# Holding the sum-free gate and up products behind the last out-projection matmul, loading their fourth operand earlier, and evacuating token tiles in one VectorE operation

## The chip, the core and the metric

The program runs on one core of one Trainium2 chip, once per launch. Its five engines work side by side, each through a queue of its own: TensorE (PE, matmuls, with its weight loads shown as PEld), VectorE (DVE), ScalarE (ACT), GpSimd (POOL) and SyncE (SP), which here only issues DMAs. ACT and POOL issue DMAs too, from the queue that also holds their arithmetic. The metric is the device time of one execution in microseconds (us), and lower is better. The kernel before took 1679.59 us, the median of three runs (1676.99 to 1682.70).

## The reference

One encoder layer over 1280 tokens (256 of a prompt, 1024 of a sample) with 1024 features. Only the second half of the layer is touched by the change:

```python
    mix = jnp.concatenate([rmsnorm(a, mla_out_g), rmsnorm(b, na_out_g)], axis=-1)
    x = x + mix @ w_o
    h2 = rmsnorm(x, ffn_norm_g)
    x = x + (jax.nn.silu(h2 @ w_gate) * (h2 @ w_up)) @ w_down
```

Everything is fp32. `a` and `b` are the outputs of the two groups of attention heads, `w_o` is 1024 x 1024, and `w_gate` and `w_up` are 1024 x 2816.

## The kernel before, in words

The tokens lie in ten tiles of 128. Each fp32 operand of a matmul is split into a high and a low part, and one product is three matmuls (high by high, high by low, low by high: lines 110 to 112, `mm3`). The high part is a ScalarE cast, the low part a subtraction on VectorE (activations) or GpSimd (weights).

**Out-projection, tile by tile** (the loop at L879). For tile t, `mix_in(t + 1)` loads the attention outputs of the next tile, scales them (rstd and scaling on GpSimd), transposes them on TensorE into the bank `trm` and splits them into `mT`. `out_proj(t)` makes 48 matmuls into `po` (two halves of 512 columns, eight contraction chunks, three matmuls each) and adds them to the residual `x` on VectorE. `ffn_in(t)` squares `x` (ScalarE, L793), takes the rstd (GpSimd), scales (VectorE, L796), transposes eight 128 x 128 blocks into `trh` or `trm` (L805) and evacuates them with the gain `gf` into the four quarters `R["11"]`, `R["12"]`, `R["21"]`, `R["22"]`. The second digit of a quarter says whether the token tile is in the first five or the last five, the first digit which half of the features it holds.

**Gate and up products.** They are made by a Strassen-Winograd scheme with seven products per pair of weight blocks in the order `SEQ = (1, 2, 6, 7, 4, 5, 3)`. Product m takes a sum of activation quarters, `S[m]`, and a sum of weight blocks. Products 1 and 2 take no sum at all: `S[1]` and `S[2]` are quarters of tiles 0 to 4, and their weights are the blocks "11" and "12" as loaded. Product 6 takes `S[6]`, which is built from the sums `T2` of tiles 5 to 9 (`build_S(6)`, five cuts of 128 tokens), and the weight sum s2 = "21" + "22" - "11" (`operand`, L858). A product is twice twelve matmuls of 320 columns (`product`, two token halves s), for the gate (i = 0) and the up projection (i = 1). `finish` applies Silu to the gate, multiplies it by up and stores finished quarters to DRAM (`act_d`, from ScalarE's queue).

In the first pass (fp = 0, L963 to L983) three of the four sum-free weights are loaded and split in the loop over token tiles, at t == 6. The fourth (block "12" of up) and the blocks for the sums go into memory that the out-projection's pools have given back, so those six loads are issued when its last matmuls are done.

**What sets the order.** The program is traced in the order of the code, and a scheduler then orders each engine's instructions by its own simulation of when operands will be there. Every engine but SP is so ordered; SP keeps the order of the code. `tc.issue_after(ins)` adds the rule that what is traced under it stands behind `ins` on the engine of `ins`. Each engine then works strictly through its own list. In the list of before, 48 of the 96 matmuls of the sum-free products stand between out-projection matmuls and 48 behind the last one.

## Time and profile before

| | before |
|---|---|
| median of three runs | 1679.59 us |
| profiled execution, its own time | 1682.38 us |
| its span in the trace | 1680.6 us |
| PE busy in the span | 1612.6 us (96%) |
| DVE, ACT, POOL busy | 888.3, 724.6, 645.3 us |
| mean granted TensorE clock | 0.985 of full speed |

The profiled execution's own time is 1.8 us above its span, and 2.8 us above the median. In the trace, times are counted from the start of the span. A view of windows gives the busy time of each engine in a stretch with the number of its instructions, the granted clock of TensorE (1.00 is 2.4 GHz) and the mean busy share of the DMA engines. A timeline row gives start, duration, engine, line and the tiles written and read; a bracket at its end is the idle time of that engine just before it and what released it. A matmul's row lasts until its result has left the array, so the spacing of starts, not the duration, is what one costs in a dense run. The busy share says where an engine works but not whether it waits for anything at the end.

### The profile page before, as it was taken

The page shows a single profiled execution, that of the slowest core. Times are in us where ns is not written, and L with a number is a line of the kernel's source. Part 1 is how long each engine was busy: PE and PEld are TensorE (multiplying, and loading weights), DVE is VectorE, ACT ScalarE, POOL GpSimd, SP SyncE. Part 2 cuts the span into 40 slices and gives each one's busy share as a digit, 9 for nine tenths or more (in the row PEclk, how much of TensorE's full clock was granted, in tenths as well). Part 3 has the DMA queues.
Part 4 walks back from the last instruction along what each step waited for, and adds up shares of the span by engine and source line. Part 5 has one row for each costly group of instructions (what it writes and reads, how often), then busy time and mean ns, then how long its engine had stood idle before and what let it go on. Part 6 is the DMA issues. An engine that isn't in the chain of part 4 may idle for free.

```text
span 1680.6 us, 25657 instructions
## 1 busy us (share of the span) xinstructions
PE 1612.6 (96%) x9601; PEld 1455.7 (87%) x9601; DVE 888.3 (53%) x1521; ACT 724.6 (43%) x1500; POOL 645.3 (38%) x795
## 2 busy tenths in 40 slices
PE   7999999999899999999969999999999999999998
PEld 6987899987688888788869999999999997788886
DVE  4654045454677777443355443344444337865776
ACT  5433144454577777544443222332222233433434
POOL 3451435353011119223367565656656650000102
PEclk9999999999999999999979999999999999999999
DMA  6635302125001003233212321322332228733434
GB/s 223 199 101 144 75 21 60 36 96 163 20 19 34 20 29 98 76 125 136 85 45 91 106 81 62 102 86 93 106 101 72 71 79 329 269 94 94 142 107 149
DMA packets 123068, 169.78 MB, mean 101 GB/s; under 512 B 35328, under 2 KB 66944, under 8 KB 122944
## 3 DMA queue, kind: packets, MB, share of 16 engines
q1 hardware_dynamic: 78704, 118.99, 23.0%
q10 hardware_dynamic: 43680, 46.87, 8.1%
q0 software_dynamic: 560, 2.29, 0.4%
q8 instruction: 75, 1.23, 0.3%
q14 instruction: 49, 0.40, 0.1%
HBM read 117.65 MB, written 50.46 MB: 100 GB/s over the span
## 4 chain that ended last, share of the span: by engine, by line
PE 83%; issue 4%; DMA 3%; POOL 3%; DVE 3%; ACT 2%; SPq 0%; ACTq 0%; POOLq 0%; DVEq 0%
PE M L112 10%; PE M L110 10%; PE M L111 10%; PE d L111 5%; PE d L110 5%; PE d L112 5%; PE o L686 3%; PE tp L679 3%; PE po L110 2%; PE pj L110 2%; PE po L112 2%; PE po L111 2%; PE pj L111 2%; PE pj L112 2%; PE na_o L462 2%
## 5 line engine op out<-in xcount | busy, mean ns | idle before, releaser
L110 PE MATMUL M<-S,wc 128*128 128x320 f32 x1056 | 324.7, 312 | 9.6 <-ACT wc L845 9.5
L111 PE MATMUL M<-S,wc 128*128 128x320 f32 x1056 | 326.7, 311 | 0.0
L112 PE MATMUL M<-S,wc 128*128 128x320 f32 x1056 | 314.0, 311 | 0.7 <-POOL wc L846 0.7
L110 PEld LDWEIGHTS M<-S,wc 128*128 128x128 f32 x1056 | 199.8, 190 | 11.4 <-ACT wc L845 11.2
L111 PEld LDWEIGHTS M<-S,wc 128*128 128x128 f32 x1056 | 200.3, 190 | 0.3
L112 PEld LDWEIGHTS M<-S,wc 128*128 128x128 f32 x1056 | 196.5, 189 | 1.6 <-POOL wc L846 1.5
L846 POOL TENSOR_TENSOR wc<-A,wc 128x512 fp32r<-128x512 f32 x85 | 119.0, 1402 | 85.6 <-ACT wc L845 84.0
L111 PE MATMUL d<-w,ah 128*128 128x512 f32 x385 | 145.8, 397 | 2.5 <-DVE w L1016 2.5
L110 PE MATMUL d<-w,ah 128*128 128x512 f32 x385 | 143.4, 397 | 3.7 <-ACT ah L1015 3.7
L112 PE MATMUL d<-w,ah 128*128 128x512 f32 x385 | 143.7, 396 | 0.0
L916 DVE TENSOR_TENSOR z<-M,z 128x320 f32<-128x320 f32 x120 | 57.0, 488 | 141.7 <-PE M L112 131.3
L845 ACT CAST wc<-A 128x512 fp32r<-128x512 f32 x85 | 52.8, 622 | 167.2 <-PE M L111 145.9
L846 POOL TENSOR_TENSOR wc<-sum,wc 128x512 fp32r<-128x512 f32 x62 | 87.8, 1415 | 86.4 <-ACT wc L845 86.4
L916 DVE TENSOR_TENSOR zB<-M,zB 128x320 f32<-128x320 f32 x100 | 47.6, 488 | 133.3 <-PE M L112 126.7
L100 DVE TENSOR_TENSOR PT<-tp,PT 128x512 fp32r<-128x512 f32 (+1 forms) x144 | 93.0, 658 | 40.8 <-ACT PT L99 39.4
L1015 ACT CAST ah<-as 128x640 fp32r<-128x640 f32 x77 | 56.0, 727 | 120.7 <-issue 65.6
L845 ACT CAST wc<-sum 128x512 fp32r<-128x512 f32 x62 | 38.4, 619 | 149.8 <-PE M L111 104.1
L99 ACT CAST PT<-tp 128x512 fp32r<-128x512 f32 (+1 forms) x144 | 79.2, 565 | 42.3 <-PE tp L679 39.4
L110 PEld LDWEIGHTS d<-w,ah 128*128 128x128 f32 x385 | 72.4, 188 | 22.2 <-ACT ah L1015 4.8
L671 DVE TENSOR_REDUCE mm<-S 128x1 f32<-128x1024 f32 (+1 forms) x80 | 84.8, 1061 | 12.8 <-PE S L112 11.2
L1016 DVE TENSOR_TENSOR ah<-as,ah 128x640 fp32r<-128x640 f32 x77 | 64.1, 835 | 51.8 <-ACT ah L1015 51.8
L111 PEld LDWEIGHTS d<-w,ah 128*128 128x128 f32 x385 | 72.5, 188 | 20.5 <-DVE w L1016 2.9
(397 smaller groups left out, 3994.0 us busy)
## 6 DMA issues: line engine op xcount, KB each, us to landing
as<-act_d SPq DMA_DIRECT2D x77, 320.0 KB
act_d<-z ACTq DMA_DIRECT2D x35, 320.0 KB
act_d<-zB ACTq DMA_DIRECT2D x35, 320.0 KB
A<-in_w_gate_dram SPq DMA_DIRECT2D x42, 256.0 KB
A<-in_w_up_dram SPq DMA_DIRECT2D x41, 256.0 KB
x<-in_x_tm_dram SPq DMA_DIRECT2D x20, 512.0 KB
cT_d<-stg ACTq DMA_DIRECT2D x20, 320.0 KB
w<-in_w_down_dram SPq DMA_DIRECT2D x11, 512.0 KB
```

The lines of the kernel that those rows point to most:

```text
L99: i = nc.scalar.copy(out=hi, in_=ps)
L100: nc.vector.tensor_sub(out=lo, in0=ps, in1=hi)
L110: nc.tensor.matmul(out, lhsT=sh, rhs=mh, start=first, stop=False, **kw)
L111: nc.tensor.matmul(out, lhsT=sh, rhs=ml, start=False, stop=False, **kw)
L112: nc.tensor.matmul(out, lhsT=sl, rhs=mh, start=False, stop=last, **kw)
L671: nc.vector.reduce_max(out=nm[:, u:u + 1], in_=S, axis=AX.X, negate=True)
L679: nc.tensor.transpose(tp[:, j], ex[:, kt * P:(kt + 1) * P], ident)
L845: i0 = nc.scalar.copy(out=hi, in_=raw)
L846: i1 = nc.gpsimd.tensor_tensor(out=lo, in0=raw, in1=hi, op=ALU.subtract)
L916: nc.vector.tensor_add(out=o, in0=ps, in1=a)
L1015: nc.scalar.copy(out=o[:, 0], in_=raw)
L1016: nc.vector.tensor_sub(out=o[:, 1], in0=raw, in1=o[:, 0])
```

## The change

- `mm3` returns its last instruction, and `out_proj` returns the last matmul of the tile. The eight sum-free products of the first pass are traced under `tc.issue_after(last_mm)`, so none of them can stand between out-projection matmuls any more. All eight come first, and the `finish` of product 2 moves to the place behind product 6.
- The block "12" of up is loaded at t == 7, into the buffer that the gate's block "12" had. Of the six late loads the blocks "21" and "22" now come first and the two blocks "12" last (the second is loaded once more for its later sum).
- `ffn_in` writes the first feature half of a tile with one VectorE multiplication (128 x 4 x 128, the gain broadcast along the tokens) and the second half with four ScalarE activations, for all ten tiles. Before, tiles 0 to 4 used four ScalarE activations for the first half and four VectorE ones for the second, and tiles 5 to 9 used eight ScalarE activations, and eight VectorE operations that subtracted into the quarters "11" and "12" on the way.
- Those subtractions are now whole-tile operations on SBUF: `difference` makes "11" and T2, `differences` makes "12" and "21". For tiles 5 to 8 these are four GpSimd operations where two stood. For tile 9 they are on VectorE, and the last two are put behind `build_S(6)`.
- `build_S(6)` no longer waits for the last difference of tile 9, so its first four cuts can be split earlier.

```diff
--- before.py
+++ after.py
@@ -109,7 +109,7 @@
         kw = {"skip_group_check": True} if onto else {}
         nc.tensor.matmul(out, lhsT=sh, rhs=mh, start=first, stop=False, **kw)
         nc.tensor.matmul(out, lhsT=sh, rhs=ml, start=False, stop=False, **kw)
-        nc.tensor.matmul(out, lhsT=sl, rhs=mh, start=False, stop=last, **kw)
+        return nc.tensor.matmul(out, lhsT=sl, rhs=mh, start=False, stop=last, **kw).ins
 
 
     p1 = pool("p1")
@@ -782,9 +782,10 @@
             hs = slice(hf * 512, (hf + 1) * 512)
             ps = po.tile([P, 512], F32, name="po", bufs=2)
             for kc in range(KC):
-                mm3(ps, mT[:, 0, kc], mT[:, 1, kc], wo[kc][:, 0, hs], wo[kc][:, 1, hs],
-                    kc == 0, kc == KC - 1)
+                last = mm3(ps, mT[:, 0, kc], mT[:, 1, kc], wo[kc][:, 0, hs], wo[kc][:, 1, hs],
+                           kc == 0, kc == KC - 1)
             nc.vector.tensor_add(out=x[:, hs], in0=ps, in1=x[:, hs])
+        return last
 
     def ffn_in(t, x):
         h2 = rm.tile([P, D], F32, name="m", bufs=3)
@@ -803,30 +804,33 @@
             for i in range(4):
                 kc = 4 * q + i
                 nc.tensor.transpose(tr[q][:, i], h2[:, kc * P:(kc + 1) * P], ident)
-            for i in range(4):
-                s = gf[:, 4 * q + i:4 * q + i + 1]
-                o = R[f"{q + 1}{t // 5 + 1}"][:, i, cs]
-                if t < 5 and q:
-                    nc.vector.tensor_scalar(out=o, in0=tr[q][:, i], scalar1=s, scalar2=1.0,
-                                            op0=ALU.mult, op1=ALU.mult)
-                else:
-                    nc.scalar.activation(o, tr[q][:, i], AF.Copy, scale=s)
-                if t >= 5:
-
-                    d = R["12" if q else "11"][:, i, cs]
-                    nc.vector.scalar_tensor_tensor(out=d, in0=tr[q][:, i], scalar=s, in1=d,
-                                                   op0=ALU.mult, op1=ALU.subtract)
+            o = R[f"{q + 1}{t // 5 + 1}"]
+            if q == 0:
+                nc.vector.tensor_mul(out=o[:, :, cs], in0=tr[q],
+                                     in1=gf[:, 0:4].unsqueeze(2).to_broadcast([P, 4, P]))
+            else:
+                for i in range(4):
+                    nc.scalar.activation(o[:, i, cs], tr[q][:, i], AF.Copy,
+                                         scale=gf[:, 4 + i:5 + i])
         if t < 5:
             split_S(1, cs)
             split_S(2, cs)
             return
-        eng = nc.vector if t == NT - 1 else nc.gpsimd
         nm = ("A21", "A22", "sum", "sum", "A12")[t - 5]
         T2[t - 5] = rY.tile([P, 4, P], F32, name=nm, bufs=2 if nm == "sum" else 1)
-        eng.tensor_tensor(out=T2[t - 5], in0=R["22"][:, :, cs], in1=R["11"][:, :, cs],
-                          op=ALU.subtract)
-        return eng.tensor_tensor(out=R["21"][:, :, cs], in0=R["21"][:, :, cs], in1=T2[t - 5],
-                                 op=ALU.subtract).ins
+        eng = nc.vector if t == NT - 1 else nc.gpsimd
+        difference(eng, R["11"][:, :, cs], R["12"][:, :, cs], R["11"][:, :, cs])
+        difference(eng, T2[t - 5], R["22"][:, :, cs], R["11"][:, :, cs])
+        if t < NT - 1:
+            differences(eng, t)
+
+    def difference(eng, out, a, b):
+        eng.tensor_tensor(out=out, in0=a, in1=b, op=ALU.subtract)
+
+    def differences(eng, t):
+        cs = slice((t % 5) * P, (t % 5 + 1) * P)
+        difference(eng, R["12"][:, :, cs], R["22"][:, :, cs], R["12"][:, :, cs])
+        difference(eng, R["21"][:, :, cs], R["21"][:, :, cs], T2[t - 5])
 
 
 
@@ -883,8 +887,10 @@
             for m, i, b in ((1, 0, "11"), (2, 0, "12"), (1, 1, "11")):
                 A0[i][b] = load_A(i, 0, b)
                 w0[m, i] = operand(A0[i], m)
-        out_proj(t, *cur)
-        last = ffn_in(t, cur[1])
+        if t == 7:
+            A0[1]["12"] = load_A(1, 0, "12")
+        last_mm = out_proj(t, *cur)
+        ffn_in(t, cur[1])
         cur = nxt
     for x in reversed(r3):
         x.release()
@@ -954,8 +960,10 @@
                 for ins in after:
                     es.enter_context(tc.issue_after(ins))
                 after = split_S(m, cs, from_)
-
-    build_S(6, (last,))
+        return after
+
+    with tc.issue_after(build_S(6, ())[1]):
+        differences(nc.vector, NT - 1)
     for fp in range(NF // 2):
         zp, zn = (rB, "zB") if fp % 2 else (l4[1], "z")
         G, U = C = [zp.tile([P, 2, NTOK], F32, name=zn, bufs=2) for _ in range(2)]
@@ -965,16 +973,16 @@
                      .rearrange("p a b -> p (a b)").rearrange("p (n a b) -> p n a b", n=5, b=P)
                      for _ in range(2)]
             at = [spare[n // 5][:, n % 5] for n in range(8)]
-            for n, (b, i) in enumerate((("12", 1), ("21", 0), ("22", 0), ("21", 1), ("22", 1),
-                                        ("12", 0))):
-                A0[i][b] = load_A(i, 0, b, at[n])
             for i in range(2):
                 for m in (1, 2):
                     for s in range(2):
-                        product(C[i], w0[m, i], m, s, held[i], 0)
-                    finish(G, U, i, m, fp)
+                        with tc.issue_after(last_mm):
+                            product(C[i], w0[m, i], m, s, held[i], 0)
                 if i == 0:
                     w0[2, 1] = operand(A0[1], 2)
+            for n, (b, i) in enumerate((("21", 0), ("22", 0), ("21", 1), ("22", 1), ("12", 0),
+                                        ("12", 1))):
+                A0[i][b] = load_A(i, 0, b, at[n])
             for n, m in enumerate(SEQ[2:]):
                 w = [operand(A0[i], m, at[6 + i], ("A21", "A22")[i]) for i in range(2)]
                 if m != 3:
@@ -982,6 +990,8 @@
                 for i in range(2):
                     for s in range(2):
                         product(C[i], w[i], m, s, held[i])
+                    if m == 6:
+                        finish(G, U, i, 2, fp)
                     finish(G, U, i, m, fp)
         else:
             for i in range(2):
```

Three places of the resulting lists are shown, with buffer numbers. In these rows `po` is an out-projection bank, `M0` and `M1` are banks of the products, `S1`, `S2` and `S6` are high and low parts of the activation sums (two numbers each), `wc` is a split weight, `S5` is the memory lent to the late loads and weight sums, and `z` holds gate and up.

On TensorE, in the middle of the out-projection (tile 6), the list of before has:

```order
L110 MATMUL po_8851<-wo7_8069,mT_8674 128x512
L111 MATMUL po_8851<-wo7_8069,mT_8674 128x512
L112 MATMUL po_8851<-wo7_8069,mT_8674 128x512
L110 MATMUL M0_9278<-S1_7998,wc_8809 128x320
L111 MATMUL M0_9278<-S1_7999,wc_8809 128x320
L110 MATMUL M0_9292<-S1_7998,wc_8809 128x320
L111 MATMUL M0_9292<-S1_7999,wc_8809 128x320
L112 MATMUL M0_9278<-S1_7998,wc_8810 128x320
```

and at the end of tile 9's out-projection, before the first product, the changed list has:

```order
L110 MATMUL po_9127<-wo7_8069,mT_9006 128x512
L806 MATMUL trh_9081<-ident_154,m_9073 128x128 x4
L806 MATMUL trm_9087<-ident_154,m_9073 128x128 x4
L111 MATMUL po_9127<-wo7_8069,mT_9006 128x512
L112 MATMUL po_9127<-wo7_8069,mT_9006 128x512
L110 MATMUL M0_9214<-S1_7998,wc_8785 128x320
L111 MATMUL M0_9214<-S1_7999,wc_8785 128x320
L112 MATMUL M0_9214<-S1_7998,wc_8786 128x320
```

The products have moved from between the `po` matmuls to behind the last one, and all 96 of their matmuls now stand there. 76 of them come before the eight transposes of tile 9 (`trh_9161`, `trm_9167`) and 20 behind; product 6 follows these. In the list of before 24 came between the last `po` matmul and the transposes of tile 9 and 24 behind.

On ScalarE, from the last evacuations of tile 9 to the weight casts of product 6 (`wc<-S5_9271` before, `wc<-S5_9213` now), the list of before has:

```order
L813 ACTIVATE zB_8005<-trm_9223,gf_8022 128x128 x2
L838 CAST S6_9256<-A12_9236 128x4x128
L845 CAST wc_9333<-S5_9270 128x512
L914 COPY z_9269<-M0_9337 128x320
L845 CAST wc_9395<-S5_9271 128x512
L914 COPY z_9269<-M0_9351 128x320
L845 CAST wc_9404<-S5_9271 128x512
L838 CAST S7_9410<-zA_8003 128x4x320 x2
L67 DMA act3_d0_84<-z_9269 128x640
L845 CAST wc_9473<-S5_9270 128x512
```

and the changed list has:

```order
L937 ACT_TABLE_LOAD
L937 ACTIVATE z_9210<-z_9210 128x640
L813 ACTIVATE zB_8005<-trm_9167,gf_8022 128x128 x4
L920 COPY z_9211<-M0_9272 128x320
L842 CAST S6_9196<-A12_9176 128x4x128
L920 COPY z_9211<-M0_9286 128x320
L67 DMA act3_d0_84<-z_9211 128x640
L849 CAST wc_9335<-S5_9213 128x512
L849 CAST wc_9344<-S5_9213 128x512
```

The store `act3_d0_84`, the first quarter of gate times up, stood behind both casts of product 6's weights and now stands in front of them. The table load and the Silu of product 2 stand in front of tile 9's evacuation `zB<-trm`.

On GpSimd, from tile 8's last differences to the low part of product 6's weight for up, the list of before has:

```order
L826 TENSOR_TENSOR sum_9147<-zB_8005,zA_8002 128x512
L828 TENSOR_TENSOR zB_8004<-zB_8004,sum_9147 128x4x128
L846 TENSOR_TENSOR wc_9334<-S5_9270,wc_9333 128x512
L856 TENSOR_TENSOR sum_9392<-S5_9270 128x512
L856 TENSOR_TENSOR sum_9401<-S5_9270 128x512
L856 TENSOR_TENSOR S5_9271<-sum_9392,A11_8807 128x512
L856 TENSOR_TENSOR S5_9270<-A11_8807,S5_9270 128x512
L856 TENSOR_TENSOR S5_9271<-sum_9401,A11_8819 128x512
L856 TENSOR_TENSOR S5_9270<-A11_8819,S5_9270 128x512
L856 TENSOR_TENSOR A21_9399<-S5_9271 128x512
L846 TENSOR_TENSOR wc_9396<-S5_9271,wc_9395 128x512
```

and the changed list, from the last difference of tile 8, has:

```order
L828 TENSOR_TENSOR zB_8004<-zB_8004,sum_9096 128x4x128
L89 TENSOR_SCALAR rh_9155<-ssh_9154 128x1
L850 TENSOR_TENSOR wc_9269<-A12_8910,wc_9268 128x512
L91 TENSOR_TENSOR rh_9155<-rh_9155,mhalf_161 128x1
L860 TENSOR_TENSOR sum_9332<-S5_9212 128x512
L860 TENSOR_TENSOR S5_9213<-sum_9332,A11_8783 128x512
L860 TENSOR_TENSOR S5_9212<-A11_8783,S5_9212 128x512
L860 TENSOR_TENSOR sum_9341<-S5_9212 128x512
L860 TENSOR_TENSOR A21_9339<-S5_9212,S5_9213 128x512
L850 TENSOR_TENSOR wc_9336<-S5_9213,wc_9335 128x512
L860 TENSOR_TENSOR S5_9213<-sum_9341,A11_8795 128x512
```

The low part of the gate's weight (`wc_9336`) now stands in front of the three sums of up, one of which (`S5_9213<-sum_9341`) is the operand of the second cast of product 6.

## Rows read from the trace of the kernel before

**Rows 1.** Windows: stretch (us from the span's start), then for PE, PEld, DVE, ACT and POOL the busy us with the number of instructions, then the granted clock, the DMA share and GB/s. The first is the whole out-projection, the second one tile of it, the third the tile in which the first weights are split; the others follow its last matmul.

```profile
700.00:836.00 136.00, 135.62 (x674) 111.41 (x675) 51.56 (x102) 57.14 (x139) 39.12 (x65) 1.00 0.30 104
...
752.00:765.00 13.00, 12.99 (x65) 10.36 (x64) 5.54 (x12) 5.84 (x14) 3.02 (x6) 1.00 0.35 122
...
778.00:792.00 14.00, 14.00 (x73) 11.66 (x72) 5.11 (x13) 6.77 (x16) 6.45 (x9) 1.00 0.49 170
...
877.00:995.00 118.00, 118.00 (x807) 118.00 (x806) 54.59 (x74) 38.23 (x64) 74.23 (x52) 1.00 0.25 82
836.00:877.00 41.00, 27.40 (x133) 24.97 (x132) 23.35 (x34) 18.78 (x36) 25.25 (x18) 0.71 0.21 73
```

**Rows 2.** Groups of instructions by line with shapes kept apart, in the stretch 700 to 836 us: count | busy us, mean ns | idle before, releaser.

```profile
L787 DVE TENSOR_TENSOR x<-po,x 128x512 f32<-128x512 f32 x19 | 13.1, 688 | 42.4 <-PE po L112 42.4
...
L810 DVE TENSOR_SCALAR zB<-trh,gf 128x128 f32<-128x128 f32 x20 | 5.6, 342 | 0.0
...
L110 PE MATMUL M<-S,wc 128*128 128x320 f32 x16 | 4.9, 308 | 0.0
...
L826 POOL TENSOR_TENSOR A<-zB,zA 128x512 f32<-128x512 f32 x2 | 2.6, 1294 | 0.0
```

**Rows 3.** Timeline of TensorE from the last out-projection matmuls on: start, us, engine, line, tiles, shape, count, and idle time before with its releaser.

```profile
836.23 0.39 PE L110 MATMUL M<-S,wc 128*128 128x320 f32 x1
...
839.68 0.31 PE L112 MATMUL M<-S,wc 128*128 128x320 f32 x1
843.46 1.09 PE L805 MATMUL trh<-ident,m 128*128 128x128 f32 x4 [3.46 <-DVE zA L817]
...
850.64 0.63 PE L110 MATMUL M<-S,wc 128*128 128x320 f32 x1 [5.25 <-ACT wc L845]
...
861.46 0.63 PE L110 MATMUL M<-S,wc 128*128 128x320 f32 x1 [2.20 <-ACT wc L845]
...
865.76 0.63 PE L112 MATMUL M<-S,wc 128*128 128x320 f32 x1 [0.23 <-POOL wc L846]
...
866.46 0.47 PE L111 MATMUL M<-S,wc 128*128 128x320 f32 x1
...
870.46 0.47 PE L110 MATMUL M<-S,wc 128*128 128x320 f32 x1
...
871.08 0.31 PE L111 MATMUL M<-S,wc 128*128 128x320 f32 x1
...
879.88 0.31 PE L111 MATMUL M<-S,wc 128*128 128x320 f32 x1
```

**Rows 4.** Who TensorE waited for between 836 and 877 us: us in total, times, longest.

```profile
PE M L110 <- ACT wc L845: 9.5, 4, 5.2
PE trh L805 <- DVE zA L817: 3.5, 1, 3.5
```

**Rows 5.** Timeline of ScalarE in that stretch, same columns: the copy of a product out of its bank, the table load and Silu of product 2, two evacuations of tile 9, the cast of S6's last cut.

```profile
840.03 0.43 ACT L914 COPY z<-M 128x320 f32<-128x320 f32 x1 [0.80 <-PE M L112]
840.47 1.28 ACT L931 ACT_TABLE_LOAD   x1
841.77 0.74 ACT L931 ACTIVATE z<-z 128x640 f32<-128x640 f32 x1
...
847.02 0.37 ACT L813 ACTIVATE zA<-trh,gf 128x128 f32<-128x128 f32 x1 [0.16 <-DVE zA L817]
847.29 0.36 ACT L813 ACTIVATE zB<-trm,gf 128x128 f32<-128x128 f32 x1
...
849.45 0.62 ACT L838 CAST S<-A 128x512 fp32r<-128x512 f32 x1 [1.01 <-DVE A L826]
```

**Rows 6.** Timeline of VectorE in that stretch: T2 and the last difference of tile 9, the first two splits of S6, the multiplication of up by gate, and the two splits of S7.

```profile
848.74 0.68 DVE L826 TENSOR_TENSOR A<-zB,zA 128x512 f32<-128x512 f32 x1
849.45 0.69 DVE L828 TENSOR_TENSOR zB<-zB,A 128x512 f32<-128x512 f32 x1
850.06 1.28 DVE L839 TENSOR_TENSOR S<-A,S 128x512 fp32r<-128x512 f32 x2
...
858.71 0.92 DVE L933 TENSOR_TENSOR z<-z 128x640 f32<-128x640 f32 x1 [3.41 <-ACT z L914]
862.60 4.46 DVE L839 TENSOR_TENSOR S<-zA,S 128x1280 fp32r<-128x1280 f32 x2 [2.97 <-ACT S L838]
```

**Rows 7.** Timeline of GpSimd in that stretch: the split of the fourth sum-free weight, one weight sum, and the split of product 6's first weight.

```profile
850.67 1.81 POOL L846 TENSOR_TENSOR wc<-S,wc 128x512 fp32r<-128x512 f32 x1 [4.43 <-ACT wc L845]
...
857.67 1.28 POOL L856 TENSOR_TENSOR S<-A,S 128x512 f32<-128x512 f32 x1
...
863.19 2.52 POOL L846 TENSOR_TENSOR wc<-S,wc 128x512 fp32r<-128x512 f32 x1
```

**Rows 8.** The chain that ended last, in order of time, where a later store stands in front of a weight cast on ScalarE's queue: start, us, what.

```profile
1001.86 0.81 DVE z L916 x2
1002.67 0.55 ACTq L67
...
1003.34 0.63 ACT wc L845
...
1004.01 0.41 PE M L110
```

**Rows 9.** The chain that ended last, inside the out-projection: four transposes at the pace of a dense run.

```profile
750.26 0.44 PE trm L776 x4
```

## The prediction

> **What bounds the kernel now.** I read the windows first [rows 1]. In the out-projection TensorE works 135.6 of 136 us at full clock, and in the gate and up stage from 877 us on 118.0 of 118: in both the matmuls are the bound. Between them, from 836 to 877 us, it is busy 27.4 of 41 us at a mean granted clock of 0.71. That stretch is where anything can be won. The reader is to see there, in TensorE's timeline [rows 3], products at 836.23 to 839.68, a wait of 3.46 us for the transposes of the last token tile, one of 5.25 us, and one of 2.20 us. The list of waits [rows 4] names the waiters' releasers: 9.5 us for ScalarE's weight casts, 3.5 us for VectorE's evacuation.
>
> What one matmul costs is read from starts in a dense run [rows 3]. Sixty starts lie between 871.08 and 879.88, so a product matmul (320 columns) costs 0.147 us at full clock. From 866.46 to 870.46 there are fifteen, 0.267 us each. That is the lower of the two levels (1.2 against 2.4 GHz), entered after the waits.
>
> I compare both lists up to the point where they become the same, inside product 7. From 836.23 the list of before has 120 product matmuls and eight transposes up to there, and the row at 871.08 is 41 matmuls ahead of it, so it is reached at 871.08 + 41 x 0.147 = 877.1. The stretch takes 40.9 us. At full clock its work would be 120 x 0.147 + 0.9 (eight transposes at 0.44 for four [rows 9]) = 18.5 us. So 22.4 us are lost to waits and the lower clock, and this is the most that the change can give.
>
> **Products moved behind the out-projection.** 48 matmuls that stood between `po` matmuls leave it. As TensorE was never idle there [rows 1], its last matmul ends 48 x 0.147 = 7.0 us earlier; the first product then starts at 829.2. I count from there as t = 0. All 96 sum-free matmuls now follow: 14.1 us, and with the transposes of tile 9 behind the 76th (at t = 11.2) TensorE is busy until t = 15.0. The 3.46 us wait for these transposes goes, and so does the one for the fourth operand, which is split long before its use at t = 10.6.
>
> **What is late next.** I walk the chain of tile 9 through the changed lists.
> - The product that Silu needs is done behind 71 matmuls, at t = 10.6. ScalarE makes two copies out of the banks (0.43 each [rows 5]) up to 11.5, then comes the table load, 1.28, and the Silu, 0.74 [rows 5], so tile 9's four evacuations start at 13.4. They follow each other by 0.27 [rows 5] and end at 14.6.
> - VectorE makes T2 (0.68, starting 0.3 behind them) until 15.5, ScalarE casts the last cut of S6 (0.62) until 16.1, and VectorE subtracts (0.64, two in 1.28) until 16.8, does the two deferred differences (0.69 each) until 18.2, and multiplies up by gate (0.92) until 19.1 [rows 5, 6].
> - The store `act3_d0_84` waits for that multiplication, and now stands in front of product 6's weight casts on ScalarE's queue. A later place in the trace shows what this does [rows 8]: the store is issued at 1002.67, as soon as VectorE is done, the cast behind it starts 0.67 later, and the matmul follows after another 0.67. So the first matmul of product 6 starts at t = 19.15 + 1.34 = 20.5, 5.5 us after TensorE ran dry.
>
> The Trainium skill, TensorE: Matmul & The Clock Gate, Architectural detail, says that ScalarE and VectorE take their queues strictly first in, first out. The trace agrees [rows 8]; by that rule, a cast that needs nothing from the store still pays for it.
>
> - After 5.25 us of idling TensorE came back at the lower level [rows 3], so I give product 6's first half 0.267 per matmul. Its four first matmuls need the high part alone; then the low part is awaited, a GpSimd split of 1.3 (alone) to 1.8 us [rows 7], to t = 21.8; twenty matmuls at 0.267 take it to 27.2.
> - GpSimd meanwhile makes three sums of up behind that split (1.28 each [rows 7]), and the split for up, 2.52 as in [rows 7] since VectorE splits S7 beside it (4.46 for two [rows 6]): 21.8 + 3.8 + 0.3 + 2.5 = 28.4. 42 matmuls remain, 6.2 us at full clock. The lists meet at t = 34.6.
>
> **The other edits cost nothing.** One VectorE multiplication of 128 x 512 from PSUM replaces four ScalarE or VectorE operations per tile. The trace does not show it; the nearest rows are 0.69 for the addition from PSUM [rows 2] at the one end and the four operations that it replaces, 4 x 0.34 [rows 2], at the other, and I take 0.69. Either hides under TensorE (VectorE works 5.5 of 13 us per tile [rows 1]), and so do two operations of 0.7 on tile 9's chain, counted above only where they end last. GpSimd gets two more differences in tiles 5 to 8, 1.29 each [rows 2]. Its load per tile rises from 3.0 us [rows 1] by 4 x 1.29 to 8.2, and to 12.1 in the tile that also splits three weights (3 x 1.3). The tile takes TensorE 13.0. So it is covered, but in that one tile only just; uncovered, it costs up to 4.1 (below). The load of the fourth operand adds one DMA in a stretch in which the DMA engines work 0.35 to 0.49 [rows 1], and a later one of the same block stays.
>
> **The sum.** 40.9 + 7.0 - 34.6 = 13.3 us. Against the profiled execution's 1682.4 (a span of 1680.6 and 1.8 around it) that is 1669.1. The median lies 2.8 us below that execution, so I forecast 1666.3.
>
> **Rivals.**
> - *The queue does not hold the cast* (the store slips by, or the multiplication is early). Then casts follow S6's last cut at t = 16.6, product 6 starts at 17.3 after a wait of only 2.3 us, at full clock, GpSimd ends the split for up at 25.2, and the lists meet at 31.4: 16.5 us gained, 1663. Against it stand [rows 8].
> - *Everything is in time.* All 168 matmuls follow at full clock, 25.6 us, 22.3 us gained, 1657. It would need sums and S6 by t = 15, and tile 9's chain alone takes longer.
> - *The clock stays low* up to the meeting point: 42 x 0.12 = 5.0 us less, 8 gained, 1671. In [rows 3] the lower level lasted to 870.5 through a row of short waits. The same time comes out if GpSimd and VectorE slow each other in the out-projection: a split of 1.3 us took 2.52 beside VectorE [rows 7]. Four differences at 2.52 make a tile 13.1 us of GpSimd, 0.1 over TensorE's, and the one with the splits 17, 4.1 over: together some 4.5 us.
>
> The Trainium skill, SBUF — State Buffer, 🔬 SBUF: two separate sides, has VectorE and GpSimd share a port pair as an exclusive lock, taken by VectorE operations with two SBUF inputs; it speaks against more GpSimd work. In the out-projection the differences took 1.29 alone, in this trace, since VectorE's inputs there are mostly PSUM [rows 2]; by the rule that remains so, except beside S6's early splits.
>
> - *No gain.* Tile 9's rstd gets late behind GpSimd's four differences of tile 8 (5.2 us, up to 10 if slowed), so the transposes hold up TensorE by 5 us, the clock falls earlier, and the walk above shifts by as much; 13.3 less 5, and less 0.12 for each of the 68 matmuls behind the transposes that I counted at full clock (8.2), leaves nothing, 1680.
> - *Slower.* The out-projection becomes GpSimd's. It decides once GpSimd needs more per tile than the 13.0 of TensorE; to eat the 13.3 us and 5 more over four tiles it must need 17.6, that is 3.6 us per difference instead of 1.29. 1685. No row shows an operation of this size above 2.52.
>
> **How the numbers follow.** Forecast 0.47, with its own range of 1662 to 1670 (the split and the multiplication 1 us earlier or later, and the spread of runs, 3 us to either side); queue does not hold 0.17; all in time 0.07; clock low or GpSimd slowed 0.15; no gain 0.09; slower 0.05. The likeliest is 1666.3. The range from 1657 to 1676 takes in the first four and leaves out the last two and a little at both ends. A change below 0.3%, 5 us, cannot be told from none here. Faster holds the first four cases with a small part lost to noise, 0.84; within 0.3% 0.10; slower 0.06.
>
> **What would show it.** In the profile of the changed kernel: out-projection matmuls without products between them and TensorE still busy all through; its last one about 7 us earlier; products without a gap for some 15 us, the transposes inside them; then one wait of about 5 us released by a weight cast, with a store on ScalarE's queue just before that cast and VectorE's multiplication before the store; matmuls at the lower level for some microseconds after it; the lists meeting at about 864. A first wait of 2 us would mean the first rival, no wait the second, gaps in front of `trm` or `trh` in tiles 6 to 9 the GpSimd ones. I am wrong if the stretch behind the out-projection is still over 40 us long, or if its end does not come earlier.

## The result and the profile after

The changed kernel took 1667.95 us (median of five runs, 1666.50 to 1671.25), the kernel before 1679.59 (five runs, 1676.99 to 1682.70): a ratio of 0.993, with a 95% interval of 0.9917 to 0.9943, so 11.6 us less. The profiled execution took 1666.5 us with a span of 1664.5.

Two profiled executions do not differ by the change alone. The stretch ahead of the out-projection is the same code in all kernels of this study, and in their 14 profiles it took between 693.5 and 700.4 us. So I use a yardstick that leaves it out: from the first `po` matmul to the last product matmul. Both times stand in the view of one tile (instructions, shortest, median and longest in ns, first and last start in us), here of before, of the changed kernel, and of the last experiment below:

```profile
L110 PE MATMUL po<-wo,mT x160: 389/394/504, 700.4 to 835.2; 128*128 128x512 f32 x160
L112 PE MATMUL M<-zA,wc x176: 305/309/309, 895.0 to 1394.5; 128*128 128x320 f32 x176
```

```profile
L110 PE MATMUL po<-wo,mT x160: 391/394/504, 695.1 to 823.3; 128*128 128x512 f32 x160
L112 PE MATMUL M<-zA,wc x176: 305/309/309, 877.0 to 1376.3; 128*128 128x320 f32 x176
```

```profile
L110 PE MATMUL po<-wo,mT x160: 391/394/504, 696.9 to 825.2; 128*128 128x512 f32 x160
L112 PE MATMUL M<-zA,wc x176: 309/309/309, 875.4 to 1374.4; 128*128 128x320 f32 x176
```

The stage takes 1394.5 - 700.4 = 694.1 us before, 681.2 in the changed kernel, 677.5 in the last one. A second profile of the changed kernel gave 680.9, so the yardstick is good to about 0.3 us, as far as one repetition can tell; the whole times of one kernel lie some 5 us apart. The kernel before has one profile, and every gain below is counted from it; two experiments on it (early fourth operand, with and without the free cuts) repeat its 135.3 us from the first to the last `po` matmul. The gain in the stage is 12.9 us. What lies behind it, from the last product matmul to the end of the span, took 286.1 us before and 288.2 after, and between these two in all 14 profiles; why it differs is not shown.

TensorE after, on the rows that answer to [rows 3] (start, us, engine, line, tiles, shape, count, idle before with its releaser):

```profile
824.67 0.39 PE L112 MATMUL po<-wo,mT 128*128 128x512 f32 x1
824.90 0.30 PE L110 MATMUL M<-S,wc 128*128 128x320 f32 x1
...
836.05 0.63 PE L806 MATMUL trh<-ident,m 128*128 128x128 f32 x4
...
839.74 0.31 PE L112 MATMUL M<-S,wc 128*128 128x320 f32 x1
845.27 0.64 PE L110 MATMUL M<-S,wc 128*128 128x320 f32 x1 [5.22 <-ACT wc L849]
...
851.33 0.41 PE L110 MATMUL M<-S,wc 128*128 128x320 f32 x1
...
852.88 0.41 PE L112 MATMUL M<-S,wc 128*128 128x320 f32 x1
```

The products run from the last `po` matmul on without a gap, tile 9's transposes among them, and one wait is left where [rows 4] had five of 13.0 us. ScalarE shows what stands in front of the cast that ends it (ACTq is a DMA issued from its queue), and VectorE and GpSimd what that in turn waits for:

```profile
836.28 1.28 ACT L937 ACT_TABLE_LOAD   x1
837.58 0.74 ACT L937 ACTIVATE z<-z 128x640 f32<-128x640 f32 x1
838.22 1.13 ACT L813 ACTIVATE zB<-trm,gf 128x128 f32<-128x128 f32 x4
...
840.63 0.62 ACT L842 CAST S<-A 128x512 fp32r<-128x512 f32 x1 [0.96 <-DVE A L828]
...
844.24 0.33 ACTq L67 DMA_DIRECT2D act_d<-z  x1
844.60 0.62 ACT L849 CAST wc<-S 128x512 fp32r<-128x512 f32 x1 [3.03 <-DVE z L939]
```

```profile
834.12 1.78 DVE L797 TENSOR_SCALAR m<-x,rh 128x1024 f32<-128x1024 f32 x1 [1.98 <-POOL rh L91]
...
842.19 0.68 DVE L828 TENSOR_TENSOR zA<-zB,zA 128x512 f32<-128x512 f32 x1
842.79 0.68 DVE L828 TENSOR_TENSOR zB<-zB,A 128x512 f32<-128x512 f32 x1
843.39 0.81 DVE L939 TENSOR_TENSOR z<-z 128x640 f32<-128x640 f32 x1
```

```profile
831.68 0.51 POOL L89 TENSOR_SCALAR rh<-ssh 128x1 f32<-128x1 f32 x1
...
834.05 1.30 POOL L860 TENSOR_TENSOR sum<-S 128x512 f32<-128x512 f32 x1
...
840.00 1.72 POOL L860 TENSOR_TENSOR A<-S,S 128x512 f32<-128x512 f32 x1
845.30 1.28 POOL L850 TENSOR_TENSOR wc<-S,wc 128x512 fp32r<-128x512 f32 x1 [3.58 <-ACT wc L849]
846.53 1.28 POOL L860 TENSOR_TENSOR S<-sum,A 128x512 f32<-128x512 f32 x1
```

The store waits for VectorE's multiplication until 844.20, and the cast behind it runs at 844.60, after ScalarE had stood idle for 3.03 us. GpSimd made its first weight sum at 834.05; in the kernel before that was at 853, behind the split of the fourth operand [rows 7]. The windows that answer to [rows 1], the first three over the same kind of stretch, the others around the wait:

```profile
700.00:826.00 126.00, 125.93 (x614) 101.55 (x614) 44.72 (x66) 47.96 (x118) 47.06 (x68) 1.00 0.34 116
752.00:765.00 13.00, 13.00 (x66) 10.64 (x65) 5.41 (x8) 6.00 (x16) 3.69 (x8) 1.00 0.35 121
778.00:792.00 14.00, 14.00 (x70) 11.38 (x69) 3.57 (x6) 7.25 (x17) 11.94 (x14) 1.00 0.49 169
...
845.30:851.30 6.00, 6.00 (x21) 5.68 (x22) 1.60 (x2) 3.45 (x4) 6.00 (x5) 0.50 0.19 74
851.30:859.10 7.80, 7.80 (x52) 7.57 (x52) 7.80 (x6) 3.58 (x5) 7.80 (x4) 0.99 0.01 2
```

GpSimd's extra work is there (11.94 of 14 us in the tile that splits the weights), and TensorE lost nothing by it. Behind the wait the granted clock is 0.50, the lower level, for a little over 6 us.

### The profile page after: what moved, and what is told of

It reads as the page before. It is cut to its first block, busy times and chain, and to the rows that moved or that the text cites. A ratio compares the mean times of both kernels' runs of the same rounds, so it can differ in the third digit from the quotient of the medians.

```text
span 1664.5 us, 25614 instructions
## 1 busy us (share of the span) xinstructions
PE 1604.7 (96%) x9601; PEld 1448.6 (87%) x9601; DVE 883.8 (53%) x1473; ACT 716.7 (43%) x1480; POOL 659.3 (40%) x803
## 3 DMA queue, kind: packets, MB, share of 16 engines
q8 instruction: 75, 1.23, 0.3%
## 4 chain that ended last, share of the span: by engine, by line
PE 82%; issue 4%; DMA 4%; DVE 4%; ACT 3%; POOL 3%; SPq 1%; ACTq 0%; POOLq 0%; DVEq 0%
PE M L110 11%; PE M L112 11%; PE M L111 11%; PE d L111 4%; PE d L112 4%; PE d L110 4%; PE o L686 3%; PE tp L679 3%; PE po L110 2%; PE po L111 2%; PE na_o L462 2%; PE po L112 2%; PE pj L110 2%; PE pj L112 2%; PE pj L111 2%
## 5 line engine op out<-in xcount | busy, mean ns | idle before, releaser
L671 DVE TENSOR_REDUCE mm<-S 128x1 f32<-128x1024 f32 (+1 forms) x80 | 84.8, 1061 | 12.7 <-PE S L112 11.0
```

Of the source, the lines that this page charges most:

```text
L671: nc.vector.reduce_max(out=nm[:, u:u + 1], in_=S, axis=AX.X, negate=True)
```

## The experiments

For each: stage is the yardstick above, gained is 694.1 less it; the time is the median, with its ratio to the kernel before on the same chip. Some expectations count from the first `po` matmul to the 300th product matmul instead. On that measure the kernel before takes 195.9 us, the changed kernel 183.2 in both of its profiles, early fourth with free cuts 187.4, cuts held 188.3, all orders 179.7, and all orders with the cast early 179.9.

| kernel | stage, us | gained | time, us | ratio, 95% interval |
|---|---|---|---|---|
| changed kernel once more | 680.9 | 13.2 | 1669.02 | 0.9929 (0.9914 to 0.9943) |
| before + hold | 695.2 | -1.1 | 1680.70 | 1.0014 (1.0002 to 1.0026) |
| changed, no hold | 681.5 | 12.6 | 1668.08 | 0.9934 (0.9914 to 0.9954) |
| before + early fourth operand | 691.1 | 3.0 | 1678.16 | 0.9992 (0.9980 to 1.0003) |
| changed, fourth operand late | 687.7 | 6.4 | 1673.53 | 0.9961 (0.9947 to 0.9975) |
| before + early fourth + free cuts | 685.7 | 8.4 | 1672.56 | 0.9954 (0.9939 to 0.9969) |
| changed, cuts held | 686.5 | 7.6 | 1672.51 | 0.9949 (0.9935 to 0.9964) |
| changed, store behind the casts | 680.9 | 13.2 | 1666.21 | 0.9929 (0.9912 to 0.9945) |
| changed, chain first | 679.6 | 14.5 | 1665.95 | 0.9922 (0.9905 to 0.9938) |
| changed, rstd first | 679.4 | 14.7 | 1665.67 | 0.9912 (0.9896 to 0.9927) |
| changed, all orders | 677.4 | 16.7 | 1666.47 | 0.9920 (0.9908 to 0.9932) |
| changed, all orders and cast early | 677.5 | 16.6 | 1662.57 | 0.9892 (0.9876 to 0.9908) |

### Which part of the change gains

**The hold.** Alone on the kernel before:

```diff
-                        product(C[i], w0[m, i], m, s, held[i], 0)
+                        with tc.issue_after(last_mm):
+                            product(C[i], w0[m, i], m, s, held[i], 0)
```

> The kernel before with one part of the change alone: the eight sum-free products held behind the last out-projection matmul. The fourth operand is still loaded, cast and split late, and the evacuation is the old one. Theory: the last out-projection matmul ends 7.0 us earlier, but what follows it hangs on the late fourth operand and on GpSimd's sums behind its split, which take their 40.9 us from that matmul as before: the whole gain is the 7.0 us, 1672.6, and a wait of about 3 us for the fourth operand stands behind some 72 product matmuls and the transposes. Rival A (holding alone does it all): 1668. Rival B (the held matmuls only fill time that the other parts make): below 2 us, 1678 to 1680.

It gained nothing and lost 1.1 us. The last `po` matmul came 1.4 us earlier than before (133.8 us behind the first, before 135.3) and not 7.0: with no products between its matmuls, transposes in the out-projection had to wait for the subtractions of the old evacuation (VectorE, L818), and the granted clock fell to 0.50 behind the longer of these waits, here as a row of TensorE and a window:

```profile
790.77 0.66 PE L806 MATMUL trh<-ident,m 128*128 128x128 f32 x4 [1.98 <-DVE zA L818]
```

```profile
792.10:795.50 3.40, 3.40 (x12) 2.82 (x11) 1.70 (x3) 1.62 (x5) 0.75 (x2) 0.50 0.78 277
```

TensorE's waits from the out-projection to the end of the stretch (for whom, us in total, times, longest):

```profile
PE M L110 <- ACT wc L846: 9.7, 4, 5.6
PE trh L806 <- DVE zA L818: 2.6, 2, 2.0
```

The waits for weight casts are those of the kernel before [rows 4]. The two for transposes lie inside the out-projection (the longer is the row at 790.77); the one in front of tile 9's transposes, 3.5 us before, is gone. GpSimd's split of the fourth operand came at 850.28, which is 151.8 us behind the first `po` matmul (before 150.3), and TensorE's wait of 5.6 us ends with the cast in front of that split. The opposite, the changed kernel without that rule:

```diff
-                        with tc.issue_after(last_mm):
-                            product(C[i], w0[m, i], m, s, held[i], 0)
+                        product(C[i], w0[m, i], m, s, held[i], 0)
```

> The changed kernel without the hold: the eight sum-free products may again stand between out-projection matmuls; early fourth operand, new evacuation and deferred differences stay. Theory: the last out-projection matmul ends up to 7 us later than in the changed kernel, fewer product matmuls cover tile 9's chain, and that chain from the scaling to product 6 (9.3 us) is what counts: the lists meet 31 to 35 us behind the last out-projection matmul, so 3 to 7 us of the 11.6 are lost, 1671 to 1675. Rival A (the hold is the whole change): 1680. Rival B (the other parts are the whole change): 1668.

It lost 0.3 or 0.6 us of stage (against 681.2 or 680.9) where 3 to 7 were expected, within or just above what the yardstick can tell. The last `po` matmul came 6.5 us later, but tile 9's rstd on GpSimd came only 2.5 us later (both from the first `po`), and product 6 not at all. Rival B of this run and rival B of the one before hold: the products fill time that other parts make.

**The fourth operand.** Alone on the kernel before (with the changed order of the six late loads):

```diff
+        if t == 7:
+            A0[1]["12"] = load_A(1, 0, "12")
         out_proj(t, *cur)
```

> The kernel before with another part of the change alone: the fourth operand loaded at t == 7 and so split early, and the six late loads in the changed order; no hold, old evacuation, old differences. Theory (GpSimd's queue): in the kernel before, the split of the fourth operand stands on GpSimd's queue in front of six sums and waits for a ScalarE cast that stands behind tile 9's evacuations, so that GpSimd is idle for 4.7 and 4.4 us; with the split gone from there the sums are made 8 to 10 us earlier, the 5.25 us wait goes, product 6 starts by the end of tile 9's old evacuation and of S6's five cuts, some 4 us earlier than before, and up's part 4 us: a gain of 4 to 7 us, 1673 to 1676. Rival A (the evacuation of tile 9 is the bound): product 6 starts no earlier, 1678 to 1680. Rival B (the fourth operand is all of the change): 1668.

It gained 3.0 us of stage, below the 4 to 7 expected, and in the time too little to tell. The number is rival A's, the cause is neither's: GpSimd's first sum was held by something else, and came 1.3 us earlier than before (counted from the first `po` matmul) and not 8 to 10.

```profile
846.05 3.31 POOL L856 TENSOR_TENSOR sum<-S 128x512 f32<-128x512 f32 x2 [5.07 <-DVE S L839]
```

And undone in the changed kernel, where the load goes back into the late ones:

```diff
-        if t == 7:
-            A0[1]["12"] = load_A(1, 0, "12")
...
+            for n, (b, i) in enumerate((("12", 1), ("21", 0), ("22", 0), ("21", 1), ("22", 1),
+                                        ("12", 0))):
+                A0[i][b] = load_A(i, 0, b, at[n])
```

> The changed kernel with the fourth operand loaded late again, as the first of seven late loads' six; hold, evacuation and differences as changed. Theory (GpSimd's queue): its split stands in front of the sums again and waits for a cast behind tile 9's evacuation and S6's last cut, so GpSimd is idle for some 6 us between tile 9's rstd and about 841 on the scale of the changed trace, TensorE waits some 5 us for the fourth operand, and the sums end at about 850 and not 842. 2 to 6 us of the 11.6 are lost: 1670 to 1674. Rival A (the sums have slack): 1668. Rival B (it is the whole change): 1678 or more.

```profile
845.13 1.27 POOL L850 TENSOR_TENSOR wc<-S,wc 128x512 fp32r<-128x512 f32 x1 [8.04 <-ACT wc L849]
```

6.5 us of the 12.9 are lost, just over the upper end of what was expected. GpSimd sits idle for 8.04 us in front of this one split, whose cast stands behind tile 9's evacuation and S6's last cut on ScalarE's queue, and six sums stand behind the split.

**The first cuts of S6.** The row at 846.05 names a VectorE split of S6 as what GpSimd waited for. The first weight sums are written into the two buffers named `sum`, and these hold the `T2` of tiles 7 and 8 until S6 is made of them. In the kernel before every cut of S6 stands behind tile 9's last difference. Early fourth operand and free cuts together, on the kernel before:

```diff
-    build_S(6, (last,))
+    build_S(6, ())
```

> The kernel before with two parts of the change: the early fourth operand with the changed load order (as in the run of that part alone), and S6's first cuts no longer held behind tile 9's last difference. In the run with the early fourth operand alone GpSimd's first sum did not start until 846.05, released by a VectorE split of S6: the sums are written into the two buffers named sum, which hold two of the T2 that S6 is made of. Theory (GpSimd was held twice, by the fourth operand's split and by these buffers): with both gone the first sums are made from about 834 to 838 on that trace's scale, product 6 waits only for tile 9's old evacuation and S6's last cut, and counted from the first out-projection matmul the 300th product matmul comes at 184 to 188 (before 195.9, fourth operand alone 193.4, changed kernel 183.2): 1668 to 1672. Rival A (the new evacuation is what the gain needs): 191 or more, 1676 to 1679.

The gain rose from 3.0 to 8.4, as the theory has it. GpSimd's sums began at 843.51, which is 841.0 on the scale of the earlier trace, and not at 834 to 838, since tile 8's old evacuation made its differences late (840.46 to 843.5), but they followed these without a wait. The line undone in the changed kernel (`last` is tile 9's `T2`):

```diff
-    with tc.issue_after(build_S(6, ())[1]):
+    with tc.issue_after(build_S(6, (last,))[1]):
```

> The changed kernel with one line undone: S6's cuts are held behind tile 9's T2 again (the hold of the products, the early fourth operand, the evacuation and the deferral stay). Theory (buffers): GpSimd's sums cannot start at 834 but only when the cuts that read the two sum buffers are split, some 7 to 8 us later, with GpSimd idle in front of them; product 6's first cast waits for them and the 300th product matmul comes 4 to 7 us later than in the changed kernel, at 187 to 190: 1672 to 1675. Rival A (the sums have slack, since the first cast is held by the store anyway): no change, 183, 1668.

```profile
845.52 1.64 POOL L861 TENSOR_TENSOR sum<-S 128x512 f32<-128x512 f32 x1 [9.60 <-DVE S L844]
```

5.3 us are lost, with GpSimd idle for 9.60 us. So the parts add up to a ladder: early fourth operand 3.0, free cuts 5.4 more (8.4), all the rest but the hold 4.2 more (12.6, the changed kernel without the hold), hold 0.3 to 0.6 more. The rest is the new evacuation, the whole-tile differences with two of tile 9's put off, and the later `finish` of product 2; no run parts these three. The fourth operand is worth 3.0 first and 6.5 last, so it pays in full only with the others in place. The free cuts are worth 5.4 behind the early fourth operand and 5.3 last; no run has them without it.

### What sets the wait that is left

**The store.** One rule more on the changed kernel:

```diff
+                if fp == 0 and n == 3:
+                    es.enter_context(tc.issue_after(cast6[0]))
                 (store_p if fp == NF // 2 - 1 else store)(act_d[n][fp], out)
```

> The changed kernel with one rule more: the store act3_d0_84 stands behind product 6's two weight casts on ScalarE's queue; nothing else moves on ScalarE. Theory (the store holds the cast): the first cast leaves right behind the copy that ends at 841.6, some 3.0 us earlier; TensorE's wait falls from 5.2 to about 2.3 us; GpSimd's split of product 6's second weight, which hangs on the first cast through a split of 1.3 and three sums of 1.3, comes 3 us earlier too, so the lists meet about 3 us earlier whatever the clock does: 1665, ratio 0.991. Rival A (the cast waits for something else, such as the last cut of S6 or the weight sum): the wait stays at about 5 us and the time at 1668. Rival B (the lower clock behind the long wait was the larger part): with the clock kept up 3 us more are gained, 1662.

The cast left at 842.25, and the whole program lies 0.7 us later in this profile, so that is 3.1 us earlier; TensorE's wait fell from 5.22 to 2.10 us. The store did hold the cast. But the stage took the same 680.9 us. VectorE and GpSimd show why:

```profile
842.97 1.80 DVE L828 TENSOR_TENSOR zA<-zB,zA 128x512 f32<-128x512 f32 x1
844.69 1.78 DVE L828 TENSOR_TENSOR zB<-zB,A 128x512 f32<-128x512 f32 x1
846.40 1.92 DVE L941 TENSOR_TENSOR z<-z 128x640 f32<-128x640 f32 x1
```

```profile
844.18 1.75 POOL L860 TENSOR_TENSOR S<-sum,A 128x512 f32<-128x512 f32 x1
845.89 1.76 POOL L860 TENSOR_TENSOR S<-A,S 128x512 f32<-128x512 f32 x1
847.61 1.86 POOL L860 TENSOR_TENSOR A<-S 128x512 f32<-128x512 f32 x1
```

In the changed kernel VectorE made its two deferred differences and the multiplication in 0.68, 0.68 and 0.81 us while GpSimd waited for the cast. With the cast released, GpSimd's sums fall beside them, and both engines slow down: up's split was late again (TensorE waited 1.97 us for it at 852.01, after 0.45 for its cast). And the lower clock came twice, behind either wait, as the windows show:

```profile
842.90:846.30 3.40, 3.38 (x11) 2.99 (x12) 3.40 (x3) 0.34 (x1) 3.36 (x3) 0.52 0.01 2
...
853.20:856.50 3.30, 3.30 (x14) 3.30 (x13) 3.30 (x5) 0.00 (x0) 3.30 (x2) 0.51 0.00 0
```

Together that is 6.7 us, where the changed kernel has a little over 6 at that level. Product 6 began 3.1 us earlier, but by the 169th product matmul, inside product 7, both kernels were in step again to 0.1 us. What the shorter wait gave was taken back.

**Tile 9's chain in front.** On top of the last one, GpSimd makes the sum of product 6's second weight ahead of the first split, and the sums of product 3 behind the splits of product 7. ScalarE makes one weight cast ahead of S6's last cut, and the table load and the Silu behind both casts (parts of the diff):

```diff
+                    with tc.issue_after(s2):
+                        w = [split_A(A0[i]["s2"]) for i in range(2)]
...
+                    with tc.issue_after(w[0][2]):
+                        cut = split_S(6, slice(4 * P, 5 * P), T2[4])
...
+                if fp == 0 and m == 2:
+                    es.enter_context(tc.issue_after(cast6[0]))
                 nc.scalar.activation(G[:, fi, cs], G[:, fi, cs], AF.Silu)
```

> The changed kernel with tile 9's chain put in front on three queues: ScalarE makes tile 9's evacuations and product 6's first weight cast before the last cut of S6, and the table load, the Silu and the store behind both casts; GpSimd makes the sum for the second weight before it splits the first, splits both, and makes the sums of products 7 and 3 behind them. Theory (what keeps product 6 back is the order on ScalarE's and GpSimd's queues and no length of work): the evacuations end at about 838.1 on the scale of the changed kernel's trace, the cast at 838.7, the last cut of S6 at 840.9; product 6 starts without a wait or within 1 us, the clock stays at 1.00, GpSimd's second split ends at about 843.5, and the lists meet 5 to 8 us earlier: 1660 to 1663. Rival A (the work itself is too long, or the engines slow each other): a wait of 2 us or more stays and the gain is below 3 us, 1665 to 1668. Rival B (what is put behind becomes late: product 7 waits for its sums or casts, or the store): the first wait goes and another of 3 us or more comes at product 7, 1665 to 1668.

Product 6 started after 1.03 us. Rival B came in part: the store now stood in front of product 7's second cast, which waited 4.08 us on ScalarE's queue for VectorE. TensorE ran product 7 without a wait even so; its waits came at the next one, product 4 (0.77 and 0.42 for VectorE, 1.33 for GpSimd). The clock did not stay at 1.00 either: from 840.9 to 844.3 us it was 0.50, with product 6's first two waits, of 1.03 and 0.98, just before and in that stretch. 1.3 to 1.6 us of stage were gained, not 5 to 8.

**The rstd of tile 9.** In the changed kernel it starts at 831.68, though ScalarE's sum of squares was done at 828.4. On the changed kernel alone:

```diff
+        if t == NT - 1:
+            with tc.issue_after(rs):
+                differences(nc.gpsimd, NT - 2)
```

> The changed kernel with tile 8's last two differences put behind tile 9's rstd on GpSimd's queue; nothing else is added or left out. In the changed trace the rstd starts at 831.68, when tile 8's four differences are done, though its sum of squares was ready at 828.4. Theory (GpSimd's queue holds tile 9 back): the rstd starts at about 828.4, the transposes of tile 9 come 3 us earlier, its chain up to S6 ends by 837 to 839, and product 6 follows the 96 matmuls with a wait of 1 to 2 us, not 5.2; behind it GpSimd's sums and splits set the pace again, so the lists meet 1 to 3 us earlier: 1665 to 1667. Rival A (tile 9's chain is hidden under the 96 matmuls): no change in the wait. Rival B (the two differences come too late for S7): a new wait in front of product 7, 1668 or slower.

TensorE's wait in front of product 6 fell to 1.19 us and the stage by 1.5 to 1.8 us, as expected. A wait of 2.69 for GpSimd's first split came behind it.

**All of it,** the last two runs in one, with product 7's casts too in front of the table load, the Silu and the store. S6's last cut keeps the place that it has in the changed kernel. Parts of its diff against the run with the chain in front:

```diff
-                    if m == 6:
+                    if m == 7:
                         finish(G, U, i, 2, fp)
...
-                if m == 6:
+                if m == 7:
-                    cast6.append(w[1][2])
+                    cast7.append(w[1][2])
```

> All orders together, on top of the changed kernel: tile 9's rstd in front of tile 8's last two differences; GpSimd makes both sums of product 6 before its two splits, then the sums and splits of product 7, and the sums of product 3 behind them; on ScalarE the casts of products 6 and 7 stand in front of the table load, the Silu and the store. In the run with the chain put first the wait at product 6 fell to 1.0 us, but ScalarE held product 7's second cast for 4.1 us behind the store, which waited for VectorE's multiplication. Theory: with this gone too, no wait from the first product to the meeting point is over 1.5 us, the clock stays at 1.00, and the lists meet 3 to 5 us earlier than in the changed kernel, counted from the first out-projection matmul: 1662 to 1665. Rival A (GpSimd's and VectorE's work is the bound, and slow beside each other): waits for GpSimd's splits of 3 us or more in all at product 7, gain below 2 us, 1666 to 1668.

No wait was longer than 1.1 us, the granted clock from 840 to 866 us was 1.00, and the stage fell by 3.5 to 3.8 us, as the theory has it. The median, 1666.47, hardly shows it, and why is not shown; in its profile 698.3 us lie ahead of the first `po` matmul, where the two of the changed kernel have 695.1 and 695.5. Last, product 6's first cast in front of the two copies that wait for the 96th matmul (its loads and sums are traced earlier for that; in the stage this cast is all that moved in the order of the work):

```diff
+                            if (i, m) == (1, 2):
+                                es.enter_context(tc.issue_after(w6[0][2]))
                             product(C[i], w0[m, i], m, s, held[i], 0)
```

> The run with all orders together, with one rule more: product 6's first weight cast stands in front of the last two copies out of the product banks on ScalarE's queue, which wait for the last of the 96 matmuls. Theory: the wait of 1.03 us in front of product 6 goes, and its first matmul follows the 96th; the 300th product matmul comes 0 to 1.5 us earlier than there (179.7), since GpSimd and VectorE set the pace behind it: 1662 to 1666. Rival A (without this first wait the clock stays up all through): 2 us or more earlier.

```profile
843.86 0.42 PE L110 MATMUL M<-S,wc 128*128 128x320 f32 x1 [1.33 <-ACT wc L852]
```

Product 6 now follows without a wait, and the 1.33 us stand in front of its first matmuls for up, whose cast waits for a GpSimd sum. Behind them the granted clock fell, as it had not in the run before:

```profile
845.40:848.90 3.50, 3.50 (x16) 3.50 (x15) 3.50 (x2) 1.00 (x2) 3.50 (x3) 0.51 0.00 0
```

So rival A fails, and the stage is the same as without this rule. The time, 1662.57 us (1661.09 to 1664.23), is below both kernels: the changed kernel beside it took 1669.02 (1666.36 to 1670.49), and the two ranges do not touch. The stage shows 3.4 to 3.7 us of the 6.5. The rest is not accounted for: the run before, with the same stage, took 1666.47 on another chip.

> The changed kernel once more, beside the others on the same chip. Theory: its stretch from the first out-projection matmul to the 300th product matmul is 183.2 us again to within 0.5 us, and its time lies within 3 us of the 1668 of the first runs, since the stretches ahead of the out-projection differ by some us from execution to execution. Rival: the stretch itself differs from execution to execution by more than 1 us, so that differences of 1 to 3 us between kernels there could not be read.

That run gave 183.2 us again, the same stage to 0.3 us, and a time 1.1 us above that of the first runs, so its theory holds.

## Why the prediction was right, and where it was not

- **Time and stretch.** 1666.3 was forecast and 1667.95 measured; 13.3 us of gain in the stretch, and 12.9 measured in the stage. In the terms of the sum it is 40.9 + 6.0 - 34.2 = 12.7: the first product behind the out-projection came 6.0 us earlier and not 7.0.
- **The walk of tile 9** held nearly step by step (t = 0 at 824.90; predicted time first). TensorE busy until 15.0: 15.2 (839.74 + 0.31). Evacuations from 13.4: 13.3. S6's last cast done at 16.1: 16.4. Its subtraction at 16.8: 17.4, since it took 0.99 and T2 1.21 us beside GpSimd. The multiplication at 19.1: 19.3. Product 6 at 20.5 after 5.5 us: 20.4 after 5.22. Up's low part at 28.4: 28.0. The lists meet at 34.6: at 852.88 + 42 x 0.147 = 859.05, which is 34.2.
- **The strict queue.** The step "a cast that needs nothing from the store still pays for it", for which the Trainium skill, TensorE: Matmul & The Clock Gate, Architectural detail, was named, is shown: the cast moved 3 us earlier when the store was put behind it. The step from there to a gain, in the rival "The queue does not hold the cast" (product 6 at 17.3, 16.5 us gained), failed. Product 6 did start at 17.3 there, but the gain was 13.2: the rival counted GpSimd's sums at their 1.28 us beside a VectorE that had just as much left to do (they took 1.75 to 1.86), and full clock, where it fell twice.
- **"Products moved behind the out-projection ... its last matmul ends 48 x 0.147 = 7.0 us earlier"** failed as a reason. The last `po` matmul came 5.7 us earlier (135.3 to 129.6 from the first), and next to nothing hangs on it: without the hold the stage is 0.3 to 0.6 us longer, and the hold alone brought that matmul 1.4 us forward and gained nothing. The sum came out because its other end, the walk, started from the right place by luck. I put tile 9's transposes at 11.2 because of their place in TensorE's list. They were ready only then: the scaling that they read ended at 835.90, t = 11.0, since GpSimd's rstd stood behind tile 8's four differences, which the walk did not count.
- **"The other edits cost nothing"** was right on cost (the new evacuation's VectorE multiplication took 0.69 us, as counted) and missed their gain. The walk contained the early cuts, and the new evacuation with what came along with it, without naming what they are worth, 5.4 and 4.2 us; that S6's cuts free the buffers of the weight sums was not seen.
- **GpSimd's load** was 11.94 us in a window of 14 with the splits in it, where 12.1 was expected in a tile of 13, and covered. The rival "No gain" had its first step right (tile 9's rstd late behind tile 8's differences): its place in the queue costs 1.5 to 1.8 us, shown by the run that moves it, and not 5, and TensorE waits for it in front of product 6, not in front of the transposes.

## What to carry to other kernels

Where an in-order engine stands idle for a long time and then does what others wait for, look for the first instruction behind the idle time and ask what that one waits for: here one split, and behind it a reused buffer, held six sums back while GpSimd stood idle for up to 9.6 us. Undo each part of a change alone and also do it alone: the part that stands first in the change's name was worth half a microsecond, and the early fourth operand 3.0 us alone and 6.5 with the rest in place. A wait that is taken away moves work beside other work; price what then runs side by side before counting the wait as gain.

## What was not expected of the hardware

Subtractions on VectorE and on GpSimd, both of 128 x 512 with two operands in SBUF, took 0.68 and 1.28 us alone, 0.60 and 1.23 from start to start (842.19 to 842.79, and 845.30 to 846.53 in the changed kernel). Side by side they took 1.80 and 1.75, and the starts on either engine lay 1.71 to 1.72 apart (842.97 to 844.69, and 844.18 to 845.89, with the store moved). One of each alone is 0.60 + 1.23 = 1.83: it looks as if they took turns, and beside each other the two engines did hardly more than one after the other. The Trainium skill, SBUF — State Buffer, 🔬 SBUF: two separate sides, has such a rule (an exclusive lock on a shared port pair, held for a whole instruction); this trace agrees with it to within 0.12 us, and does not show the lock itself.

The clock fell behind short waits too: with the store moved TensorE was without work for 2.10 us, and the granted clock behind that was 0.52, in the main the lower level, for 3.4 us. In the last run it was 0.51 for 3.5 us behind a wait of 1.33. With all orders it stayed at 1.00 through waits of 1.03 and 1.08.
